# Layer 0 of a two-layer decoder: two differential heads moved ahead of the sparse heads' projections, a sparse pair moved to the end

## The chip, the cores and the metric

One core of one Trainium2 chip runs the whole program. The metric is the time of one execution on the device in microseconds (us). The kernel before takes 1274.81 us, the median of three runs (1271.99 to 1275.66). TensorE (PE in the rows) multiplies matrices and also transposes, PEld is its loading of weights, VectorE is DVE, ScalarE is ACT, GpSimd is POOL, and SyncE (SP) issues all transfers here.

## The reference

Two post-norm decoder layers over 512 tokens of width 1024, in float32. Only layer 0's mixer is touched by the change:

```python
h = x @ w_in_even[li]
qa, ka, va, qn, kc, vc, ksl, vsl, kw, vw, g = _split(h, EVEN_SPLITS)
o_a = diff_attention(...)   # 4 heads: softmax 0 minus lam * softmax 1, times v; RMS norm
o_b = nsa_attention(...)    # 8 query heads in 2 groups: compressed keys, selected keys, window
mix = jnp.concatenate([o_a, o_b], axis=-1) @ w_out_even[li]
x = layer_norm(ALPHA * x + mix, ...)
x = layer_norm(ALPHA * x + sqrelu_mlp(x, ...), ...)
```

The four differential heads and the eight sparse heads don't depend on each other. A differential head needs its own q and k columns of `h` and the v columns of its pair of heads. A sparse head needs its group's q, the compressed keys and values (made from `kc`, `vc` by a small MLP over windows of 32 tokens), two more pairs of k and v, and the gates `g`. With 512 tokens the selection keeps all blocks, so the second and the third branch are plain causal attention. Layer 1 is a forgetting attention of 16 heads and another MLP; its code and its place stay as they are.

## The kernel before

Matmuls run in a float32 format that keeps fewer bits, so each operand is split into a high and a low part (`split`, L112; `unit`, L130) and each product takes three matmuls (L180 to L182). A projection of 256 columns ("chunk") is 96 matmuls of 128x256, in two PSUM banks of 48. Its weights come as two transfers of 512 KB into `wraw` (two buffers, `RB`), ACT makes the high part (L144) and DVE or POOL the low part (L145).

Layer 0's attention is a list of tasks, recorded in the order of `EVEN_ORDER` (L39):

- `W`: projects the inputs of the compression and lays out windows (in two buffers of tag "p"); `C`: the compression MLP, whose weights `w1` come in eight transfers of 512 KB into buffers of tag "v" (four in all, L681); it reads the windows, and its matmuls are full float32 (L687).
- `Q0`, `Q1`: the q of a sparse group (four buffers of tag "q", six in all). `B0`, `B1`: k and v of the second and third branch, the gates with `B1`. Their v take one "v" buffer each for the rest of the attention.
- `c0`, `c1`: the compressed branch's softmax of a group. `P00`, `P01`, `P10`, `P11`: a pair of sparse heads (group, pair): four softmaxes, then `fold` (L306) and `split_y` (L312) into a row block of the output projection's operand.
- `D0` to `D3`: q and k of a differential head. `V01`, `V23`: v of two such heads (two "v" buffers each). `H0` to `H3`: the head itself, two softmaxes, their difference, the product with v, the norm.

A softmax (L262) is, for four blocks of 128 queries, two matmuls into a bank of tag "s", a masked minimum on DVE (L274) and an exp on ACT (L275); it takes one of two "p" buffers. `scale_p` (L316) scales three blocks on POOL (L321) and one on DVE (L323). `transpose_p` (L278) is ten transposes on TensorE (L288), each group of them split into two parts by ACT (L114) and DVE (L116). `stacks_q` and `stacks_k` (L233, L250) split the transposed q and k out of PSUM. `rope` (L564) turns 16 of 64 channels in eight small operations for two blocks of tokens.

PSUM has two banks under each of four tags: "g" for projections and the output projection, "s", "t" and "o". The transposes of a differential head's q and k go to tags that depend on the head (L904): head 0 "g" and "g", head 1 "o" and "g", head 2 "t" and "g", head 3 "t" and "s".

```python
for k in EVEN_ORDER:
    if k == "c0":
        lo_engine[0] = rope_engine[0] = G
    ...
    elif k[0] == "D":
        got[k] = diff_qk(*['gg', 'og', 'tg', 'ts'][int(k[1])])
    ...
    if k in _EVEN:
        ahead()
```

Up to `c0` the low parts of weights (L145) and the rope run on DVE, from there on on POOL. `ahead()` (L607) fetches and splits the weights two chunks ahead. The first two chunks of the list are fetched before the attention (L1031 to L1037).

The list is not the order of execution. A scheduler takes the recorded instructions and sets, for each engine, one fixed order by its own model of time, with buffers given out as they come free; on the chip each engine works through its own list in that order and waits at an instruction whose inputs are not there. So the matmuls of the projections stand between those of the heads. The matmuls of the output projection's first half (L335 to L337) need the first four row blocks in the order in which `EVEN_ORDER` finishes them (`EVEN_KBS`, L45); they are evacuated at L340 with the input x added. The second half (L357 to L359) needs the other four, then follow the layer norm and the MLP.

Of the kernel before, what the change touches and what calls it, by code (L numbers as in the profile page):

```python
# [35 lines left out]

EVEN_ORDER = "W C Q0 B0 B1 c0 D1 V01 P01 P00 D0 Q1 H0 c1 H1 P10 D3 P11 D2 V23 H3 H2".split()  # L39
_EVEN = {"W": [(2048, 256)], "B0": [(2304, 256)], "B1": [(2560, 280)], "Q0": [(1536, 256)], "Q1": [(1792, 256)],  # L40
         "V01": [(1024, 256)], "V23": [(1280, 256)]}
for _h in range(4):
    _EVEN[f"D{_h}"] = [(128 * _h, 128), (512 + 128 * _h, 128)]
EVEN_CHUNKS = [_EVEN[k] for k in EVEN_ORDER if k in _EVEN]
EVEN_KBS = [{"H": 0, "P": 4}[k[0]] + (int(k[1:], 2) if k[0] == "P" else int(k[1])) for k in EVEN_ORDER if k[0] in "HP"]  # L45
FOX_GROUPS = [3, 0, 1, 2]
# [14 lines left out]
def tile_trunk(ctx: ExitStack, tc: tile.TileContext, x, xt_in, ln_gain, ln_bias, w_up, w_down, w_ie, w_oe, lam_p, subln,  # L61
# [539 lines left out]
    def even_attention(ap, mh, ml):  # L601
# [289 lines left out]
        got = {}  # L891
        for k in EVEN_ORDER:
            if k == "c0":
# [241 lines left out]
```

## Time and profile before

| what | us |
|---|---|
| median of three runs | 1274.81 |
| the profiled execution, its whole time | 1273.6 |
| its span, first to last instruction | 1271.5 |
| PE busy | 1237.5 (97%) |
| PEld busy | 1079.2 (85%) |
| DVE busy | 878.2 (69%) |
| ACT busy | 647.3 (51%) |
| POOL busy | 301.2 (24%) |

The chain that ended last is PE for 86% of the span. Matmuls overlap in the pipeline, so a PE that counts as busy may still run thin; the weight loads of the same matmuls, one each, show that better: where PEld is idle, TensorE was waiting between matmuls. Layer 0's attention and the first part of its output projection take the first 308 us of the span. TensorE's granted clock is 0.994 of full speed over the whole span.

### The profile page before, as it was taken

The page shows a single profiled execution, that of the slowest core. Times are in us where ns is not written, and L with a number is a line of the kernel's source. Part 1 is how long each engine was busy: PE and PEld are TensorE (multiplying, and loading weights), DVE is VectorE, ACT ScalarE, POOL GpSimd, SP SyncE. Part 2 cuts the span into 40 slices and gives each one's busy share as a digit, 9 for nine tenths or more (in the row PEclk, how much of TensorE's full clock was granted, in tenths as well). Part 3 has the DMA queues.
Part 4 walks back from the last instruction along what each step waited for, and adds up shares of the span by engine and source line. Part 5 has one row for each costly group of instructions (what it writes and reads, how often), then busy time and mean ns, then how long its engine had stood idle before and what let it go on. Part 6 is the DMA issues. An engine that isn't in the chain of part 4 may idle for free.

```text
span 1271.5 us, 18398 instructions
## 1 busy us (share of the span) xinstructions
PE 1237.5 (97%) x7046; PEld 1079.2 (85%) x7046; DVE 878.2 (69%) x1602; ACT 647.3 (51%) x1185; POOL 301.2 (24%) x321
## 2 busy tenths in 40 slices
PE   7999998998999999999998999999999999999997
PEld 7999897898988888888887889889988888888886
DVE  5476768787859478495456788879767948669454
ACT  5266766764355454454423576767334445354530
POOL 1125565354200000000044354556510000000012
PEclk9999999999999999999999999999999999999999
DMA  7321121034414405234014322323630522505201
GB/s 274 114 87 54 34 67 35 5 129 138 167 61 132 133 25 175 67 96 146 17 50 150 101 84 92 92 88 129 231 112 23 182 84 68 164 34 159 73 17 50
DMA packets 46758, 125.15 MB, mean 98 GB/s; under 512 B 4672, under 2 KB 5184, under 8 KB 46672
## 3 DMA queue, kind: packets, MB, share of 16 engines
q1 hardware_dynamic: 46672, 123.99, 30.3%
q8 instruction: 55, 0.90, 0.3%
q14 instruction: 31, 0.25, 0.1%
HBM read 119.75 MB, written 4.23 MB: 98 GB/s over the span
## 4 chain that ended last, share of the span: by engine, by line
PE 86%; DVE 6%; DMA 3%; ACT 2%; issue 1%; POOL 1%; SPq 0%; DVEq 0%; ACTq 0%; POOLq 0%
PE g L193 11%; PE g L194 11%; PE g L195 11%; PE g L180 4%; PE g L181 4%; PE g L182 4%; PE s L478 3%; PE t L288 3%; PE s L479 3%; PE s L480 2%; DMA wraw<-w_up 2%; PE s L270 2%; PE o L480 2%; PE t L478 2%; PE o L478 2%; PE o L479 2%
## 5 line engine op out<-in xcount | busy, mean ns | idle before, releaser
L194 PE MATMUL g<-big,wlo 128*128 128x512 f32 x608 | 236.8, 391 | 0.0
L195 PE MATMUL g<-big,whi 128*128 128x512 f32 x608 | 236.6, 390 | 0.0
L193 PE MATMUL g<-big,whi 128*128 128x512 f32 x608 | 236.3, 390 | 0.0
L144 ACT ACTIVATE whi<-wraw 128x1024 fp32r<-128x1024 f32 (+3 forms) x120 | 125.3, 1045 | 112.5 <-DMA wraw<-w_up 37.1
L212 POOL TENSOR_TENSOR ve<-ve,nhalf 128x1 f32<-128x1 f32 x16 | 15.9, 991 | 647.0 <-DVE ve L211 647.0
L145 DVE TENSOR_TENSOR wlo<-wraw,whi 128x1024 fp32r<-128x1024 f32 (+2 forms) x69 | 84.3, 1228 | 96.5 <-ACT whi L144 96.4
L145 POOL TENSOR_TENSOR wlo<-wraw,whi 128x1024 fp32r<-128x1024 f32 (+2 forms) x51 | 123.4, 2425 | 94.6 <-ACT whi L144 82.3
L195 PEld LDWEIGHTS g<-big,whi 128*128 128x128 f32 x608 | 114.2, 188 | 23.6
L193 PEld LDWEIGHTS g<-big,whi 128*128 128x128 f32 x608 | 114.2, 188 | 23.2 <-issue 0.2
L194 PEld LDWEIGHTS g<-big,wlo 128*128 128x128 f32 x608 | 114.1, 188 | 23.1
L180 PE MATMUL g<-whi,big 128*128 128x256 f32 (+2 forms) x416 | 120.3, 289 | 0.6 <-DVE fz L946 0.4
L182 PE MATMUL g<-whi,big 128*128 128x256 f32 (+2 forms) x416 | 119.6, 287 | 0.0
L181 PE MATMUL g<-wlo,big 128*128 128x256 f32 (+2 forms) x416 | 119.1, 286 | 0.0
L414 DVE TENSOR_TENSOR wlo<-wdr,whi 128x1024 fp32r<-128x1024 f32 x72 | 87.4, 1218 | 44.4 <-ACT whi L413 44.4
L275 ACT ACTIVATE p<-p,sm 128x128 f32<-128x128 f32 (+3 forms) x160 | 89.2, 558 | 45.7 <-DVE sm L274 44.5
L395 ACT ACTIVATE big<-g 128x512 f32<-128x512 f32 x64 | 38.2, 597 | 134.4 <-PE g L195 134.4
L413 ACT ACTIVATE whi<-wdr 128x1024 fp32r<-128x1024 f32 x72 | 75.9, 1055 | 48.2 <-PE t L480 29.6
L321 POOL TENSOR_TENSOR p<-p,rs 128x128 f32<-128x128 f32 (+2 forms) x108 | 71.5, 688 | 93.2 <-DVE rs L970 40.4
L180 PEld LDWEIGHTS g<-whi,big 128*128 128x128 f32 x416 | 79.1, 190 | 2.2 <-ACT fv L114 0.6
L182 PEld LDWEIGHTS g<-whi,big 128*128 128x128 f32 x416 | 79.1, 190 | 0.7 <-issue 0.4
L181 PEld LDWEIGHTS g<-wlo,big 128*128 128x128 f32 x416 | 79.1, 190 | 0.6
L116 DVE TENSOR_TENSOR ptl<-t,pth 128x384 fp32r<-128x384 f32 (+1 forms) x108 | 63.1, 595 | 21.1 <-ACT pth L114 20.4
(313 smaller groups left out, 3093.0 us busy)
## 6 DMA issues: line engine op xcount, KB each, us to landing
wraw<-w_up SPq DMA_DIRECT2D x64, 512.0 KB, 3.7
wdr<-w_down SPq DMA_DIRECT2D x64, 512.0 KB, 4.7
wraw<-w_io SPq DMA_DIRECT2D x22, 512.0 KB, 3.3
wraw<-w_ie SPq DMA_DIRECT2D x18, 512.0 KB, 3.7
v<-w SPq DMA_DIRECT2D x8, 512.0 KB, 5.2
wraw<-w_oe SPq DMA_DIRECT2D x8, 512.0 KB, 3.6
cb<-c_dram SPq DMA_DIRECT2D x16, 256.0 KB, 3.2
wraw<-w_oo SPq DMA_DIRECT2D x8, 512.0 KB, 3.4
```

Of the source, the lines that this page charges most:

```text
L144: A.activation(hi[:, c], raw[:, c], AF.Copy)
L145: (eng or lo_engine[0]).tensor_tensor(lo[:, c], raw[:, c], hi[:, c].bitcast(F32), op=ALU.subtract)
L180: T.matmul(bv[:, tt], xh, h, start=first, stop=False)
L181: T.matmul(bv[:, tt], xh, l, start=False, stop=False)
L182: T.matmul(bv[:, tt], xl, h, start=False, stop=last)
L193: T.matmul(b[:, a:e], h[:, cs], xh, start=k == 0, stop=False)
L194: T.matmul(b[:, a:e], l[:, cs], xh, start=False, stop=False)
L195: T.matmul(b[:, a:e], h[:, cs], xl, start=False, stop=k == 7)
L275: A.activation(pv, pv, AF.Exp, bias=sm[:, i:i + 1], scale=-1.0, accum_out=sm[:, 4 + i:5 + i])
L413: A.activation(hi, r, AF.Copy)
L414: V.tensor_tensor(lo, r, hi.bitcast(F32), op=ALU.subtract)
L478: T.matmul(bv, hh, us[m][0][:, k], start=first, stop=False, skip_group_check=True)
```

## The change

One line, the list of tasks:

```diff
-EVEN_ORDER = "W C Q0 B0 B1 c0 D1 V01 P01 P00 D0 Q1 H0 c1 H1 P10 D3 P11 D2 V23 H3 H2".split()
+EVEN_ORDER = "D0 V01 D1 H0 W C H1 Q0 B0 B1 c0 P00 D2 P01 V23 H2 Q1 c1 P10 D3 H3 P11".split()
```

The host packs the weights by the same list, so each chunk still is one contiguous block, now in another order. The first two chunks fetched are those of D0 and V01 instead of W and Q0. The point from which rope and low parts run on POOL (`c0`) comes after D0, V01, D1, W, Q0, B0 and B1 instead of after W, Q0, B0 and B1: the ropes of D0 and D1 and the low parts of six more units of weights run on DVE. The first half of the output projection takes H0, H1, P00 and P01 instead of P01, P00, H0 and H1; the last block is P11 instead of H2, and its low part is made by DVE (L822).

No instruction is added on TensorE. What stands where, on the engines:

TensorE at the end of the first projection, before. `g_34` is the second bank of W, `t_36` and `t_40` take its transposes, `g_66` is the first bank of the second chunk, Q0:

```order
L181 MATMUL g_34_206<-big_11_85,big_6_74 128x256
L182 MATMUL g_34_206<-big_11_85,big_7_75 128x256
L623 MATMUL t_36_260<-ident_2_69,nat_33_204 128x128 x2
L623 MATMUL t_40_278<-ident_2_69,nat_33_204 128x128 x2
L180 MATMUL g_66_431<-big_14_120,big_4_72 128x256
L181 MATMUL g_66_431<-big_14_120,big_4_72 128x256
```

The same place now. `g_36` is the second bank of D0, `g_40` and `g_43` take the transposes of its q and k, `g_56` is the first bank of the second chunk, V01; `nat_33` and `nat_37` are the two halves of D0 after the rope:

```order
L181 MATMUL g_36_217<-big_11_85,big_6_74 128x256
L182 MATMUL g_36_217<-big_11_85,big_7_75 128x256
L623 MATMUL g_40_279<-ident_2_69,nat_33_204 128x128 x2
L623 MATMUL g_43_290<-ident_2_69,nat_33_204 128x128 x2
L623 MATMUL g_40_279<-ident_2_69,nat_37_266 128x128
L623 MATMUL g_43_290<-ident_2_69,nat_37_266 128x128
L623 MATMUL g_40_279<-ident_2_69,nat_37_266 128x128
L623 MATMUL g_43_290<-ident_2_69,nat_37_266 128x128
L180 MATMUL g_56_321<-big_14_120,big_4_72 128x256
```

Before, the second chunk's matmuls followed two pairs of transposes into "t"; now they follow all eight, and both banks of tag "g" are taken by the transposes.

DVE at the same place, now: the rope of D0's second half (L575 to L579) ends here, L145 makes the low parts of D1's weights, L246 and L258 empty `g_40` and `g_43`:

```order
L579 TENSOR_TENSOR nat_37_266<-rp1_38_269,rp2_39_270 128x4x16 x2
L145 TENSOR_TENSOR wlo_50_310<-wraw_48_307,whi_49_309 128x1024
L145 TENSOR_TENSOR wlo_53_316<-wraw_51_313,whi_52_315 128x1024
L246 TENSOR_TENSOR q_41_284<-g_40_279,q_41_284 64x512
L246 TENSOR_TENSOR nka_44_295<-g_43_290,nka_44_295 64x512
L258 CAST nkb_45_296<-nka_44_295 64x512
L246 TENSOR_TENSOR q_42_287<-g_40_279,q_42_287 64x512
L246 TENSOR_TENSOR nka_46_301<-g_43_290,nka_46_301 64x512
```

Before, DVE stood here with the low parts of V01's counterpart and a copy for W out of "t" (`y_38`), and no projection's bank waited for it:

```order
L145 TENSOR_TENSOR big_15_121<-wraw_17_126,big_15_121 128x1024
L667 COPY y_38_266<-t_36_260 64x511
L145 TENSOR_TENSOR wlo_46_299<-wraw_44_296,whi_45_298 128x1024
L145 TENSOR_TENSOR wlo_49_305<-wraw_47_302,whi_48_304 128x1024
L667 COPY y_39_272<-t_36_260 64x511
```

Bank `g_40` now comes free at the second L246 of q, behind two L145.

TensorE where the first half of the output projection runs out, before. `g_688` is its last bank, `o_633` takes H3's transposes, `g_715` is the first bank of the second half, `t_648` and `t_651` belong to H2:

```order
L335 MATMUL g_688_3884<-whi_685_3853,big_18_130 128x256
L336 MATMUL g_688_3884<-wlo_686_3854,big_18_130 128x256
L887 MATMUL o_633_3518<-ident_2_69,ft_626_3475 128x128
L337 MATMUL g_688_3884<-whi_685_3853,big_19_131 128x256
L887 MATMUL o_633_3518<-ident_2_69,ft_626_3475 128x128
L357 MATMUL g_715_3955<-whi_694_3917,big_20_132 128x256
```

The same place now, in the middle of P10; `o_515` is P10's second head, `g_716` the second bank of the second half, `s_567` to `s_570` are H3's first softmax:

```order
L337 MATMUL g_688_3884<-whi_685_3853,big_19_131 128x256
L357 MATMUL g_715_3955<-whi_694_3917,big_20_132 128x256
...
L303 MATMUL o_515_2978<-pth_546_3093,v_225_1465 128x128
L304 MATMUL o_515_2978<-ptl_547_3094,v_225_1465 128x128
L357 MATMUL g_715_3955<-whi_694_3917,big_20_132 128x256
L358 MATMUL g_715_3955<-wlo_695_3918,big_20_132 128x256
L357 MATMUL g_716_3982<-whi_700_3929,big_20_132 128x256
L358 MATMUL g_716_3982<-wlo_701_3930,big_20_132 128x256
L270 MATMUL s_567_3264<-nka_563_3256,q_559_3242 128x128
L271 MATMUL s_567_3264<-nkb_564_3257,q_559_3242 128x128
```

Before, the product of H3 was done when the first half ran out, and one head was left. Now all of H3 and all of P11 are left, with 36 matmuls of the second half among them.

## Rows read from the trace of the kernel before

**Rows 1.** Windows: length, busy PE, PEld, DVE, ACT, POOL, granted clock, DMA
```profile
34.00:91.00 57.00, 56.80 (x478) 56.06 (x478) 32.81 (x115) 22.09 (x53) 7.72 (x15) 1.00 0.30 98
91.00:127.40 36.40, 36.24 (x281) 34.32 (x279) 22.26 (x60) 23.18 (x58) 20.80 (x30) 1.00 0.19 59
127.40:142.20 14.80, 12.93 (x82) 9.96 (x80) 13.15 (x37) 12.64 (x33) 10.95 (x20) 1.00 0.22 73
142.20:199.10 56.90, 56.90 (x463) 56.11 (x462) 37.94 (x109) 37.77 (x96) 32.10 (x61) 1.00 0.12 38
199.10:234.60 35.50, 29.93 (x179) 23.96 (x176) 31.81 (x95) 27.16 (x79) 14.98 (x17) 0.95 0.10 31
271.00:292.40 21.40, 21.40 (x175) 21.14 (x175) 19.75 (x51) 13.77 (x39) 8.83 (x7) 1.00 0.26 75
292.40:308.10 15.70, 12.06 (x78) 10.29 (x77) 9.64 (x21) 6.72 (x18) 5.18 (x5) 0.89 0.22 62
```

**Rows 2.** PE in order of time at 127 and 142 us: start, us
```profile
127.41 0.38 PE L623 MATMUL g<-ident,nat 128*128 128x128 f32 x2
...
142.16 0.36 PE L180 MATMUL g<-whi,big 128*128 128x256 f32 x1
```

**Rows 3.** PE in order of time, where the first chunk ends
```profile
21.34 0.60 PE L623 MATMUL t<-ident,nat 128*128 128x128 f32 x4
21.69 0.36 PE L180 MATMUL g<-big,big 128*128 128x256 f32 x1
```

**Rows 4.** ACT in order of time, 15 to 27 us
```profile
16.27 2.00 ACT L144 ACTIVATE big<-wraw 128x1024 fp32r<-128x1024 f32 x2
21.54 0.60 ACT L654 ACTIVATE nat<-g 128x512 f32<-128x512 f32 x1 [3.27 <-PE g L182]
```

**Rows 5.** DVE in order of time, 15 to 25 us
```profile
17.36 1.23 DVE L145 TENSOR_TENSOR big<-wraw,big 128x1024 fp32r<-128x1024 f32 x1 [1.96 <-ACT big L144]
...
18.63 1.22 DVE L145 TENSOR_TENSOR big<-wraw,big 128x1024 fp32r<-128x1024 f32 x1
```

**Rows 6.** DVE by line and form, 20 to 100 us: busy, mean ns
```profile
L579 DVE TENSOR_TENSOR nat<-rp,rp 128x64 f32<-128x64 f32 x4 | 0.9, 217 | 0.0
```

**Rows 7.** DMA issues of the page: KB, us to landing
```profile
wraw<-w_ie SPq DMA_DIRECT2D x18, 512.0 KB, 3.7
v<-w SPq DMA_DIRECT2D x8, 512.0 KB, 5.2
```

**Rows 8.** DVE by line and form, 100 to 345 us
```profile
L310 DVE TENSOR_TENSOR y<-o,ft 64x512 f32<-64x512 f32 x8 | 5.5, 682 | 0.8 <-ACT ft L309 0.8
...
L258 DVE CAST nkb<-nka 64x512 fp32r<-64x512 f32 x8 | 3.4, 422 | 0.3
...
L145 DVE TENSOR_TENSOR wlo<-wraw,whi 128x1024 fp32r<-128x1024 f32 x2 | 2.4, 1217 | 0.0
...
L246 DVE TENSOR_TENSOR q<-g,q 64x512 fp32r<-64x512 f32 x2 | 1.4, 688 | 0.1
```

**Rows 9.** PE in order of time, after a wait near the end of H2
```profile
296.22 0.43 PE L357 MATMUL g<-whi,big 128*128 128x256 f32 x1 [2.11 <-DVE big L340]
296.45 0.41 PE L358 MATMUL g<-wlo,big 128*128 128x256 f32 x1
```

**Rows 10.** DVE by line, 199 to 234 us
```profile
L274 DVE CUSTOM_DVE_ANT_0 p<-s,K 128x128 f32<-128x128 f32 (+3 forms) x23 | 10.6, 474 | 1.7 <-PE t L288 0.9 <-PE s L271 0.6
L116 DVE TENSOR_TENSOR ptl<-t,pth 128x384 fp32r<-128x384 f32 (+1 forms) x15 | 8.6, 595 | 0.0
```

**Rows 11.** POOL in order of time, 283 to 296 us
```profile
283.66 2.39 POOL L145 TENSOR_TENSOR wlo<-wraw,whi 128x1024 fp32r<-128x1024 f32 x1 [5.67 <-issue]
286.22 1.99 POOL L321 TENSOR_TENSOR p<-p,rs 128x128 f32<-128x128 f32 x3 [0.17 <-DVE rs L853]
```

**Rows 12.** DVE line L853: xcount, duration ns min/median/max, first and last start
```profile
L853 DVE TENSOR_SCALAR rs<-rs,lam x4: 218/230/1578, 166.5 to 284.5; 128x4 f32<-128x4 f32 x4
```

**Rows 13.** DVE in order of time, 284 to 286 us
```profile
284.50 1.58 DVE L853 TENSOR_SCALAR rs<-rs,lam 128x4 f32<-128x4 f32 x1
```

## The prediction, made before the changed kernel was run

> **What bounds the kernel now.** I read the page first: PE is busy for 97% of the span and is 86% of the chain that ended last, so a saving on another engine counts only where PE runs thin. Since matmuls overlap in the pipeline, I looked for thin places by PEld, which has one weight load for each matmul: its idle time inside a stage is time that TensorE lost there. The windows of the attention [rows 1] show three kinds of stage. From 142.2 to 199.1 us PEld is idle for 56.9 - 56.11 = 0.79 us and 463 matmuls pass, 0.123 us each: TensorE sets the pace. From 127.4 to 142.2 it is idle for 14.8 - 9.96 = 4.84 us: between the transposes at 127.41 and the next matmul of a projection at 142.16 [rows 2], D0's transposes hold both banks of tag "g", so nothing of a projection can run. From 199.1 to 234.6 it is idle for 35.5 - 23.96 = 11.54 us: this is H1 and P10 without a matmul of a projection between them, and DVE, busy for 31.81 of 35.5 us (90%), sets the pace. The stage at the end, 292.4 to 308.1, loses 15.7 - 10.29 = 5.41 us, in which H2 ends alone. So PE's loss in the attention is a matter of where softmaxes stand without a projection's matmuls beside them, and the change decides just that.
>
> **The change part by part.** TensorE gets the same instructions in another order, and from the second half of the output projection on the order is as before. So I sum the lost time that goes and the lost time that comes.
>
> *What goes.* The three stages above leave the order: D0's transposes no longer stand at 127, H1 and P10 now have matmuls of other tasks among theirs, and H2 isn't last. 4.84 + 11.54 + 5.41 = 21.8 us. TensorE's own work in them stays.
>
> *What comes, a: the front.* Now D0 is first. Before, the second chunk started at 21.69, when TensorE had put W's transposes into "t" [rows 3]. Now both "g" banks are D0's transposes, and V01's first matmul waits until DVE has emptied the first. Its chain: D0's last matmul ends like W's, at 21.34 [rows 3]; ACT's copy ends at 21.54 + 0.60 = 22.1 [rows 4]; the rope of the second half is 8 operations of 0.217 us [rows 6], to 23.9; four more transposes take the 0.35 us of rows 3, to 24.3. But on DVE two L145 for D1's weights stand ahead of the evacuation. They need a `wraw` buffer, free when DVE has finished the L145 of the second chunk at 17.36 + 1.23 = 18.6 and 18.63 + 1.22 = 19.85 [rows 5]; a landing takes 3.7 us [rows 7], so 22.3 and 23.6; ACT's high part takes 1.0 (2.00 for two [rows 4]), so 23.3 and 24.6; DVE, done with the rope at 23.9, ends the L145 at 25.1 and 26.3. Then come L246 for q, L246 for k, the cast L258 and the second L246 of q, 0.69 + 0.69 + 0.42 + 0.69 [rows 8], to 28.8. V01 starts at 28.8 instead of 21.69: 7.1 us, less 0.35 for transposes that TensorE did later before. To the 6.8 comes the clock. After a wait of 2.11 us matmuls of 256 columns came 0.23 us apart (296.22 to 296.45 [rows 9]) and not 0.12, and in that stage the granted clock was 0.89 [rows 1]: 2 x 0.11 x 15.7 = 3.5 us at the lower level (1.2 for 2.4 GHz), half of them lost, 1.7. I take 8.5. The lower bound leaves the two L145 out of the way and the clock up: 26.1 - 21.69 = 4.4. The upper lets these transfers take the 5.2 us of w1's [rows 7], 1.5 more: 10.
>
> *b: shorter stretches without a projection.* Counted in the new order of TensorE, four stretches of 26 to 34 rows have softmaxes or heads alone, 118 rows together. The stretch from 199 to 234.6 has 138 rows and lost 11.54 us, 0.084 each: 118 would lose 9.9. But one of 27 rows in the order of before lies in the stage from 142.2 to 199.1, which lost 0.79 in all [rows 1]. A short one is bridged by work already queued. I take half, 5, with 0 and 9.9 as ends.
>
> *c: the tail.* H3 and P11 now stand after the first half of the output projection, with 36 of its second half's matmuls among them. They are six softmaxes: 24 of L274 and 16 of L116. The stretch from 199 to 234.6 has 23 and 15 [rows 10], so I take its loss, 11.5. Behind it stands the drain of the last block, which nothing covers: POOL's scaling of 1.99 [rows 11], the last transposes and their split, L310 of 0.68 [rows 8], the two halves of the split for the output projection. Part of this chain was at the end of H2 too. I estimate 3.5 us more than what the stretch holds, and take 15. The ends are 11.5 (no drain) and 20 (twice the drain, and the clock once more).
>
> The sum is 8.5 + 5 + 15 - 21.8 = **+6.7 us**. The profiled execution took 1273.6, so 1280.3; it lies 1.2 under the median of 1274.8, against which I forecast 1281.5. The low ends give 4.4 + 0 + 11.5 - 21.8 = -5.9, or 1269; the high ones 10 + 9.9 + 20 - 21.8 = +18, or 1293.
>
> *Moved at no price.* The ropes of D0 and D1 (16 operations of 0.217 each, 3.5 us a head) and six L145 of 1.22 go from POOL to DVE in the front. There DVE is busy for 32.81 of 57 us [rows 1], and this fills it without making it the bound, but for the two L145 in (a). If that cover is gone, 7 to 14 us of DVE would stand in the way. On SP's queue six transfers of w1 stand behind two "v" buffers that V01 used to take later; the transfer behind them is D2's second unit, many chunks ahead of its use.
>
> *A rule that speaks for the change.* POOL's L145 ran from 283.66 to 286.05 (2.39 us [rows 11]), and DVE's L853, an operation on four numbers with a median of 0.230, took 1.58 and ended at 286.08 [rows 12, 13]. So a POOL operation can hold up DVE for its length. The Trainium skill, "SBUF — State Buffer", section "Who interferes with whom", states it as a lock: the two engines share a pair of ports, and the one that starts first keeps it for the whole instruction while the other fully blocks. The row agrees in this instance; the other three L853 escaped. By the rule six L145 less on POOL could spare DVE at most 6 x 1.35 = 8.1 us, and at the average over the four L853 (a third) some 2.5; where DVE paces TensorE, the sum would then be +4.2. I leave it out of the sum, since these six leave the stages in which TensorE sets the pace.
>
> **The rivals.** *A, faster.* Heads start on DVE long before the sparse projections end, so DVE may be far ahead by the tail and TensorE not thinned there. In the stage from 271 to 292.4, also with H3 in it, PEld lost 21.4 - 21.14 = 0.26 us [rows 1]. With that and the drain the tail costs 4 instead of 15, and the sum is -4.3: 1270.5. It decides if DVE is busy under some 80% of the tail (in 271 to 292.4 it was 19.75 of 21.4, 92%, but with projections' matmuls to fill TensorE). Against it: six softmaxes need their minima and splits inside the tail, and those matmuls are gone.
>
> *B, no change.* The wait in front costs 1 instead of 8.5, because TensorE there waits for the first weights in any case and V01's later start is made up in a later wait for weights; the sum is -0.8: 1274. For it: in the first 34 us everything waits for transfers. Against it: V01's weights are there before the banks are, and from 34 us on PEld lost just 0.94 in 57 us [rows 1], so there is nothing later to give back.
>
> *C, much slower.* C now runs with V01 alive in two of the four "v" buffers, so w1's eight transfers use two. One pair's matmuls must end before the next lands, 5.2 us [rows 7] against the little that is in between; at 3.5 us exposed for each of three pairs that is +10.5 on my sum: 1292. It decides if no other work stands between the pairs. For it: H1, whose softmaxes want the "p" buffers that hold C's windows, can't fill in. Against it: B0 and Q0 can be placed there.
>
> **How the numbers follow.** The forecast has a chance of 0.45, with a range of its own of 1276 to 1287; A 0.24, B 0.20, C 0.11. About 0.3%, 3.8 us, can be told from no change. A and nothing else is faster: 0.24. B is the same: 0.20. The forecast and C are slower: 0.56. The range for 8 in 10 goes from 1269 to 1293, by the sums of the low and the high ends, and leaves out the better half of A and the worse half of C.
>
> **What would show it.** Of (a): V01's first L180 at about 29 us, with PE waiting for DVE's L246 and a granted clock under 1 behind it. Of the part that goes: no stretch of 14 us at both "g" banks, none of 35 us without a projection around 200. Of (b): PEld's loss inside the four short stretches, 0 to 10 us in all. Of (c): the last 36 us of the attention with PEld idle for about 15 and DVE busy for 90%, and POOL's scaling in the chain at the end. The attention would then end near 315 instead of 308. The forecast is wrong if PEld loses less than 5 us in that tail (A), if V01 starts before 24 us (B), or if PE waits on w1 for more than 8 us (C).

## The result, and the profile after

The changed kernel takes 1324.72 us (median of 4 runs), the kernel before 1275.24 beside it: ratio 1.0395, 95% interval 1.0369 to 1.042. It is slower by some 49.5 us, where +6.7 was forecast; the time lies 32 us above the range.

The windows of both kernels up to the end of the second half of the output projection (columns as in [rows 1]), of before and then of after:

```profile
0.00:328.00 328.00, 309.14 (x2362) 292.37 (x2363) 229.78 (x612) 192.46 (x467) 137.85 (x199) 0.99 0.30 100
328.00:1271.50 943.50, 928.34 (x4687) 786.85 (x4685) 648.42 (x990) 454.88 (x718) 163.34 (x123) 1.00 0.31 98
```
```profile
0.00:378.00 378.00, 335.61 (x2356) 312.89 (x2357) 233.40 (x651) 195.28 (x468) 112.88 (x160) 0.90 0.26 87
378.00:1323.50 945.50, 929.12 (x4692) 787.92 (x4690) 648.48 (x992) 454.57 (x718) 163.32 (x123) 1.00 0.29 98
```

Of the 50 us in this part, 65.11 - 35.63 = 29.5 are idle time of PEld, and 312.89 - 292.37 = 20.5 are the same weight loads (2357 and 2363 records) taking longer: the granted clock fell from 0.99 to 0.90. Behind this part 2 us differ. So two columns hold the whole difference: how long TensorE waits between matmuls, and how long it then runs at the lower clock.

Where TensorE waits, in six windows of after; the third row is no wait but the stretch behind one:

```profile
20.97:28.99 8.02, 1.59 (x11) 0.90 (x10) 5.94 (x15) 6.10 (x10) 0.00 (x0) 0.85 0.58 196
117.56:140.95 23.39, 13.06 (x60) 10.12 (x58) 17.33 (x78) 9.36 (x28) 1.39 (x2) 0.60 0.07 23
140.95:146.01 5.06, 5.06 (x22) 5.06 (x22) 3.54 (x10) 2.87 (x7) 0.00 (x0) 0.50 0.00 0
237.19:271.00 33.81, 28.19 (x163) 24.89 (x161) 21.94 (x61) 18.10 (x50) 11.61 (x16) 0.77 0.32 110
302.14:310.77 8.63, 3.88 (x26) 2.92 (x24) 7.20 (x10) 5.49 (x10) 1.66 (x1) 0.95 0.23 64
313.83:339.26 25.43, 22.09 (x107) 17.39 (x107) 21.07 (x67) 17.30 (x57) 7.20 (x11) 0.74 0.00 0
344.29:356.31 12.02, 7.69 (x38) 5.92 (x38) 5.99 (x14) 6.09 (x14) 1.96 (x3) 0.86 0.00 1
```

PEld is idle for 7.1 us in front, 13.3 at 117 to 141, 8.9 at 237 to 271 and 5.7 + 8.0 + 6.1 = 19.9 in the tail. That is 49.2 us; less the 21.8 us that the prediction saw go, it makes 27.4 of the 29.5. In the front, TensorE in order of time (what [rows 3] show of before):

```profile
28.99 0.55 PE L180 MATMUL g<-big,big 128*128 128x256 f32 x1 [5.40 <-DVE q L246]
29.34 0.41 PE L181 MATMUL g<-big,big 128*128 128x256 f32 x1
29.56 0.41 PE L182 MATMUL g<-big,big 128*128 128x256 f32 x1
```

V01 starts at 28.99 (28.8 was forecast), and its matmuls start 0.22 us apart. The largest new wait, at 117 to 141, is 29 rows of TensorE's order long, like the short stretches of the prediction's term b, but nothing like this size was forecast for it. TensorE, then ACT, in that stretch:

```profile
118.85 0.65 PE L704 MATMUL o<-pch,ft 128*64 128x64 f32 x8 [1.00 <-DVE ft L700]
123.67 0.37 PE L719 MATMUL t<-ident,ft 64*128 64x64 f32 x1 [4.17 <-DVE ft L716]
...
132.68 0.66 PE L887 MATMUL o<-ident,ft 128*128 128x128 f32 x2 [0.83 <-DVE ft L884]
...
139.77 0.45 PE L623 MATMUL o<-ident,nat 128*128 128x128 f32 x1 [0.80 <-DVE nat L579]
```
```profile
138.15 0.38 ACT L738 ACTIVATE nat<-g 128x256 f32<-128x256 f32 x1 [0.89 <-PE o L623]
```

In order of time these are the end of C (L704, L719), then H1's product and norm (L887), then Q0's transposes (L623), each a short step that waits for DVE, and all in "o" or "t". ACT can copy B0's bank (L738) only when these transposes have freed a "nat" buffer, so both "g" banks stay full and the projection of B1, broken off at 117.56, goes on at 140.95, at a clock of 0.50 until 146. C stands there because it is late: before, its matmuls of L687 started at 34.2 to 48.9 us. POOL laying out the compression's windows, the transfers of w1 on SP, and C's matmuls (duration in ns, first and last start):

```profile
80.93 1.46 POOL L670 TENSOR_TENSOR p<-y,pe 128x256 f32<-128x256 f32 x2 [17.18 <-issue]
```
```profile
89.97 17.14 SPq L683 DMA_DIRECT2D v<-w  x6
```
```profile
L687 PE MATMUL t<-p,v x128: 217/275/275, 88.0 to 113.2; 128*128 128x64 f32 x128
```

The windows take both "p" buffers, which H0 has until its transposes, from 72 us on; six transfers of w1 go out between 90 and 107 as pairs of "v" buffers come free; H1's softmaxes need "p" again when C has read it.

What this does to the order shows in counts. Instructions of the exps (L275, two for each of 96 blocks of queries), before (all done by 300) and after, stretch by stretch:

```profile
0.00:140.00 140.00, 15.01 (x48) 1.00 0.38 128
140.00:200.00 60.00, 15.55 (x48) 1.00 0.11 36
200.00:240.00 40.00, 15.11 (x48) 0.96 0.09 27
240.00:300.00 60.00, 15.35 (x48) 0.97 0.27 89
```
```profile
0.00:140.00 140.00, 10.29 (x32) 0.91 0.35 116
140.00:200.00 60.00, 11.12 (x36) 0.92 0.16 54
200.00:240.00 40.00, 10.95 (x35) 1.00 0.15 53
240.00:300.00 60.00, 13.28 (x42) 0.86 0.21 71
300.00:360.00 60.00, 15.24 (x48) 0.81 0.11 34
```

At 240 us before has 24 blocks left, after 45; and after has no matmul of the projections left there (L180 from 240 to the end of the attention: none; before 21, and as many of L181 and of L182). From then on only the output projection's matmuls stand beside softmaxes.

### The profile page after: what moved, and what is told of

It is laid out like the page before. It is cut to its first block, busy times and chain, and to the rows that moved or that the text cites. A ratio compares the mean times of both kernels' runs of the same rounds, so it can differ in the third digit from the quotient of the medians.

```text
span 1323.5 us, 18399 instructions
## 1 busy us (share of the span) xinstructions
PE 1264.7 (96%) x7046; PEld 1100.8 (83%) x7046; DVE 881.9 (67%) x1641; ACT 649.8 (49%) x1185; POOL 276.2 (21%) x282
## 4 chain that ended last, share of the span: by engine, by line
PE 80%; DVE 6%; ACT 2%; DMA 1%; issue 1%; POOL 0%; DVEq 0%; SPq 0%; ACTq 0%; POOLq 0%
PE g L193 11%; PE g L194 11%; PE g L195 11%; PE t L288 3%; PE s L478 3%; PE g L180 3%; PE s L479 2%; PE g L182 2%; PE g L181 2%; PE s L480 2%; PE o L479 2%; PE o L478 2%; PE t L478 2%; PE o L480 2%; PE s L270 2%; PE s L271 2%
## 5 line engine op out<-in xcount | busy, mean ns | idle before, releaser
L144 ACT ACTIVATE whi<-wraw 128x1024 fp32r<-128x1024 f32 (+3 forms) x120 | 125.5, 1046 | 108.4 <-DMA wraw<-w_up 29.5
L145 DVE TENSOR_TENSOR wlo<-wraw,whi 128x1024 fp32r<-128x1024 f32 (+2 forms) x75 | 90.9, 1215 | 100.8 <-ACT whi L144 100.5
L145 POOL TENSOR_TENSOR wlo<-wraw,whi 128x1024 fp32r<-128x1024 f32 (+2 forms) x45 | 108.4, 2412 | 89.9 <-ACT whi L144 83.2
L180 PE MATMUL g<-whi,big 128*128 128x256 f32 (+2 forms) x416 | 122.7, 295 | 1.4 <-ACT nat L654 1.0
L275 ACT ACTIVATE p<-p,sm 128x128 f32<-128x128 f32 (+3 forms) x160 | 89.2, 558 | 68.0 <-DVE sm L274 67.0
L181 PE MATMUL g<-wlo,big 128*128 128x256 f32 (+2 forms) x416 | 121.1, 291 | 0.0
L182 PE MATMUL g<-whi,big 128*128 128x256 f32 (+2 forms) x416 | 120.6, 290 | 0.0
L180 PEld LDWEIGHTS g<-whi,big 128*128 128x128 f32 x416 | 80.9, 194 | 4.1 <-ACT nat L654 1.3
L181 PEld LDWEIGHTS g<-wlo,big 128*128 128x128 f32 x416 | 80.9, 194 | 0.9 <-issue 0.4
L182 PEld LDWEIGHTS g<-whi,big 128*128 128x128 f32 x416 | 80.7, 194 | 0.7 <-issue 0.4
L116 DVE TENSOR_TENSOR ptl<-t,pth 128x384 fp32r<-128x384 f32 (+1 forms) x108 | 63.2, 596 | 22.6 <-ACT pth L114 21.8
```

Of the source, the lines that this page charges most:

```text
L144: A.activation(hi[:, c], raw[:, c], AF.Copy)
L145: (eng or lo_engine[0]).tensor_tensor(lo[:, c], raw[:, c], hi[:, c].bitcast(F32), op=ALU.subtract)
L180: T.matmul(bv[:, tt], xh, h, start=first, stop=False)
L181: T.matmul(bv[:, tt], xh, l, start=False, stop=False)
L182: T.matmul(bv[:, tt], xl, h, start=False, stop=last)
L275: A.activation(pv, pv, AF.Exp, bias=sm[:, i:i + 1], scale=-1.0, accum_out=sm[:, 4 + i:5 + i])
```

## The experiments

All medians stand beside runs of the kernel before on the same chip; "ratio" is to before. Two versions are compared by their medians, and the medians of before beside them go from 1272.9 to 1275.2. So a difference between two versions is known to some 4 us: the 5.5 of e3 and the 2.8 of g2 below shrink to 3.1 and 1.2 when each is taken against its own runs of before, and are not clear of that; those of e1 and e4 hardly are.

**Front and tail by themselves.** `e2_d0_ts`:

```diff
-['gg', 'og', 'tg', 'ts']
+['ts', 'og', 'tg', 'ts']
```

> The changed kernel, but D0's transposes go to the banks t and s instead of both g. Theory: V01's first matmul no longer waits for DVE's evacuation, it starts at 22 to 23 us instead of 29.0, the clock doesn't fall there, and the time falls by 8 to 11, to 1314 to 1317. Rival (the front is bound by the transfers of the weights, the wait only moves to D1's or W's weights): the start moves but the time falls by less than 4.

Measured: 1314.51, ratio 1.0317 (1.0292 to 1.0342), 10.2 less than the changed kernel. The first matmul of V01 follows D0's transposes at once, at full clock:

```profile
20.21 0.38 PE L623 MATMUL s<-ident,nat 128*128 128x128 f32 x2
20.35 0.36 PE L180 MATMUL g<-big,big 128*128 128x256 f32 x1
```

So the wait for the "g" banks cost some 10, near the 8.5 forecast. `e5_tail_only`, on the kernel before:

```diff
-... H1 P10 D3 P11 D2 V23 H3 H2
+... H1 P10 D2 V23 H2 D3 H3 P11
```

> The kernel before, with its list changed only behind P10: D2 V23 H2 D3 H3 P11 instead of D3 P11 D2 V23 H3 H2, so that H3 and P11 end the attention as in the changed kernel. Theory (the new tail costs on its own what stands in the changed kernel from 302 to 356 us, about 20 us of idle weight loads and 11 us of granted clock, less the 11.5 and 4 of the stretches that before has): 8 to 18 us slower than before, 1283 to 1293. Rival A (the tail costs nothing once the front is as before, since DVE is ahead): within 4 us of before. Rival B (P11 as the last task saves the drain of H2): faster by 3 or more.

Measured: 1289.58, ratio 1.0124 (1.01 to 1.0148), 16.7 slower than before, as the theory said. The two stretches at its end:

```profile
279.50:300.63 21.13, 17.30 (x97) 13.10 (x95) 17.96 (x63) 14.37 (x50) 7.54 (x12) 0.92 0.09 25
305.91:320.32 14.41, 10.20 (x46) 7.20 (x45) 7.45 (x21) 7.13 (x19) 1.96 (x3) 0.75 0.00 0
```

In them PEld is idle for 8.0 + 7.2 us, much like in the last two windows of the changed kernel (8.0 and 6.1). The tail is a cost of its own.

**The stretch at 117 to 141.** `e1_natb`, with two "nat" buffers for the other tasks instead of three (`NB = 2`) and in `branch`:

```diff
-tl = new(ap, "nat", [P, 2, 256], bufs=NB)
+tl = new(ap, "natb", [P, 2, 128], bufs=2)
```

> The changed kernel, but k of the sparse branches B0 and B1 is copied into two buffers of its own (natb) and the other tasks share two of nat instead of three. Theory 1 (in the stretch from 117.6 to 141.0 us no projection can run because the copy of B0's and B1's banks waits for a nat buffer, which Q0's transposes free only after H1's product has left the o banks): the stretch without a projection goes down from 23.4 to under 12 us and the time by 8 to 15, to 1310 to 1317. Rival 1 (TensorE's list itself puts the end of C, H1's product and norm and Q0's transposes in a row, whatever the buffers): a stretch of 20 us or more stays, time 1320 to 1330.

Measured: 1317.13, ratio 1.0347 (1.0318 to 1.0375), 7.6 less. But the stretch stayed:

```profile
121.10:147.15 26.05, 18.03 (x84) 15.44 (x83) 18.55 (x82) 10.68 (x31) 1.39 (x2) 0.56 0.00 0
```

It is 26.05 us long with 26.05 - 15.44 = 10.6 idle: the time just misses theory 1, the stretch speaks for rival 1. The "nat" buffer alone doesn't make the stretch. Where the 7.6 us come from is not shown, since two things were changed at once.

`e3_h1_late` (list: `... H0 W C Q0 B0 B1 c0 H1 P00 ...`):

> The changed kernel with H1 behind c0 in the list instead of ahead of Q0. Theory (H1's product and norm, chained with the end of C and Q0's transposes, make the stretch from 117.6 to 141.0 us, 13.3 us of idle weight loads and a clock at half for 24 us): the stretch goes and the time falls by 15 to 22, to 1303 to 1310. Rival (two softmaxes and a product need their time on DVE wherever they stand, and the stretch only moves): falls by less than 6.

Measured: 1319.25, ratio 1.0372 (1.0334 to 1.0409), 5.5 less, not clear of noise: the rival. The stretch shrank to C's end and the transposes behind it, and another one, 15.5 us long, came at 224; 7.5 + 7.0 us are idle in the two:

```profile
114.47:124.14 9.67, 3.84 (x22) 2.19 (x20) 8.41 (x54) 2.29 (x8) 0.00 (x0) 0.66 0.00 1
224.11:239.65 15.54, 10.66 (x67) 8.54 (x65) 12.04 (x40) 11.31 (x33) 7.03 (x9) 1.00 0.53 198
```

`e8_w1_once`: the eight products of C read one loaded block of w1 (`if j == 0 and c == 0:` ahead of the tile and its DMA), so seven of the eight transfers are left out.

> The changed kernel, but only the first of w1's eight blocks is loaded and used for all eight products of C (the output is wrong by that; the matmuls are the same). Theory 3 (C runs from 88 to 113 us instead of 34 to 49 because it has two v buffers and its transfers come one pair at a time, so that its end and H1 come when the sparse projections are used up): the stretch without a projection at 117 to 141 us goes, and the time falls by 12 to 22, to 1303 to 1313. Rival (the p buffers alone set C's and H1's start, the transfers only spread C among projections that run anyway): falls by less than 6, to 1319 or more.

Measured: 1312.35, ratio 1.0301 (1.0259 to 1.0342), 12.4 less. C's matmuls and what is left of the stretch:

```profile
L687 PE MATMUL t<-p,v x128: 217/275/275, 88.3 to 103.5; 128*128 128x64 f32 x128
```
```profile
120.00:133.58 13.58, 7.62 (x42) 5.62 (x40) 10.46 (x45) 6.84 (x23) 1.39 (x2) 0.74 0.25 78
```

C's last matmul starts at 103.5 instead of 113.2, and 13.3 us of idle become 8.0: the stretch shrank, but it did not go. `g1_c_early` (`D0 D1 W C V01 H0 H1 Q0 ...`) and `g3_c_early_ts` (the same with D0 in "t" and "s") give C its four buffers in another way:

> The changed kernel with W and C ahead of V01 and H0 (D0 D1 W C V01 H0 H1 Q0 B0 B1 ...), so that C has four v buffers and the p buffers for itself, and the two heads still stand ahead of the other sparse projections. Theory 3 (the windows wait 19.6 us for H0's p buffers, C is late, H1 waits for C): the serial stretch goes and the time falls by 12 to 22, to 1303 to 1313. Rival (heads 0 and 1 must stand somewhere without projections beside them, as the run with the sparse projections first showed): within 6 of 1325.

> The same with D0's transposes in t and s. Theory: another 8 to 11 us less than with both in g, as on the changed kernel. Rival (with C early the front's wait is covered): less than 3 us of difference.

Measured: 1313.05, ratio 1.0297 (1.0264 to 1.033), 11.7 less; and 1308.68, ratio 1.0259 (1.0224 to 1.0295), 4.4 less again. C in g1 and the stretch behind it:

```profile
L687 PE MATMUL t<-p,v x128: 217/275/294, 66.4 to 81.4; 128*128 128x64 f32 x128
```
```profile
118.39:130.70 12.31, 7.03 (x43) 5.36 (x40) 8.52 (x29) 7.03 (x23) 1.38 (x2) 0.76 0.12 39
```

In g1 V01's place is taken by D1, whose first matmul starts at 26.70, 2.3 us earlier than V01 did, so less was to be won there with "t" and "s", and some 2 us of g1's 11.7 belong to the front. C's lateness costs 9 to 12 us, by two edits that differ.

**The middle.** `f2_sparse_first` (`W C Q0 B0 B1 c0 D0 V01 H0 D1 H1 P00 D2 ...`):

> The changed kernel with W C Q0 B0 B1 c0 put back ahead of the differential heads (then D0 V01 H0 D1 H1 and the rest as changed), so that only the head of the list is undone. Theory (the front with the wait at D0 costs 10, the serial stretch at H1 and its like in the middle some 20, and both come from the differential heads ahead of the sparse projections): it falls to 1287 to 1297, close to the 1289.6 of the kernel before with the new tail alone. Rival (the middle's loss comes from the mixing of the other heads, D2 V23 H2 among P00 and P01): 1303 to 1312, only the front's 10 us are won.

Measured: 1326.96, ratio 1.041 (1.0393 to 1.0428): nothing won. My theory and its rival both fell. With the sparse projections back in front, PEld is idle for 8.9 and 12.5 us in two other stretches, at D0's transposes into "g" and at the heads behind their own projections; that these are the same loss moved is a reading, not shown by an edit:

```profile
90.70:101.27 10.57, 2.50 (x16) 1.65 (x14) 3.24 (x6) 5.23 (x10) 6.61 (x10) 0.66 0.31 99
143.85:183.23 39.38, 29.92 (x189) 26.86 (x187) 26.96 (x67) 22.08 (x61) 17.87 (x22) 0.87 0.17 54
```

`g2_ahead` (`D0 V01 D1 W C H0 Q0 B0 B1 H1 c0 D2 P00 V23 P01 Q1 H2 c1 D3 P10 H3 P11`):

> The changed kernel with each projection one head further ahead of its use (D0 V01 D1 W C H0 Q0 B0 B1 H1 c0 D2 P00 V23 P01 Q1 H2 c1 D3 P10 H3 P11). Theory 4 (the loss of the middle is the chain from a projection through rope, transposes and split to the first softmax, exposed where a head follows its projection at once): the time falls by 10 or more, below 1315. Rival (the projections are used up earlier still, and the last heads stand alone for longer): 1322 to 1340.

Measured: 1321.91, ratio 1.0359 (1.0321 to 1.0397), 2.8 less, which is no difference: theory 4 fell too, and the rival is missed by 0.1. `e4_old_tail` (changed up to P00, then `P01 Q1 c1 P10 D3 P11 D2 V23 H3 H2`), and `h1_both` (the same tail behind g3's front):

> The changed kernel with its list behind P00 as before: P01 Q1 c1 P10 D3 P11 D2 V23 H3 H2 instead of D2 P01 V23 H2 Q1 c1 P10 D3 H3 P11. Theory (front, middle and tail add up; the new tail alone cost 16.7 us on the kernel before): the time falls by 12 to 20 from the changed kernel's 1324.7, to 1305 to 1313. Rival (the loss of the middle is handed on to whatever tail there is): within 6 us of the changed kernel, 1319 or more.

> The run with C early and D0 in t and s (1308.7), its list behind P00 as before: P01 Q1 c1 P10 D3 P11 D2 V23 H3 H2. Theory 5 (the losses sit in separate places: front, C and H1, tail, each with its own price): the time falls by 12 to 20, to 1289 to 1297, and 14 to 22 over the kernel before are left for the sparse pairs that start late. Rival (one loss handed on: with 16 of 96 softmax blocks done at 140 us instead of 24, the rest must run without projections at some place): falls by less than 7, as on the changed kernel (5.7).

Measured: 1318.99, ratio 1.0347 (1.0324 to 1.0369), 5.7 less than changed; and 1299.32, ratio 1.019 (1.0158 to 1.0222), 9.4 less than g3. Both fall short of the 16.7 that the tail costs alone, e4 into its rival, h1 between the two: the prices of the places don't add up, and part of a loss is handed on. e4 loses 6.6 + 13.3 us in two stretches of its middle:

```profile
203.77:227.84 24.07, 21.52 (x140) 17.45 (x138) 20.47 (x62) 18.96 (x53) 9.36 (x15) 1.00 0.00 1
238.65:273.67 35.02, 28.66 (x135) 21.71 (x135) 27.44 (x76) 21.94 (x58) 13.76 (x17) 0.78 0.10 30
```

`h2_mix`, on the kernel before:

```diff
-... P01 P00 D0 Q1 H0 c1 H1 P10 D3 P11 D2 V23 H3 H2
+... P01 P00 D0 H0 H1 D2 V23 H2 Q1 c1 P10 D3 P11 H3
```

> The kernel before with only the other heads mixed: H0 H1 D2 V23 H2 ahead of Q1 c1 P10, then D3 P11 H3 at the end. Theory 5 (the differential heads' short softmaxes use up the projections D2, V23 and Q1 early, and P10, P11 and H3 stand alone): 15 to 30 slower than before, 1289 to 1304, with a stretch without a projection of 40 us or more at the end. Rival (mixing costs nothing, what costs is the front and P11 as last task): within 6 of before.

Measured: 1298.41, ratio 1.0187 (1.0163 to 1.021), 23.8 slower, by the order of the heads alone (which also makes H3 the last task instead of H2). The same counts of L275 as above; then those of L180 from 200 to 240, before and in h2; then the last two stretches without a projection, with a short piece of the output projection between them:

```profile
0.00:140.00 140.00, 14.98 (x48) 1.00 0.37 128
140.00:200.00 60.00, 14.93 (x48) 0.91 0.11 36
200.00:240.00 40.00, 6.22 (x20) 0.96 0.20 69
240.00:300.00 60.00, 16.93 (x52) 0.91 0.17 61
```
```profile
200.00:240.00 40.00, 3.15 (x11) 2.14 (x12) 0.96 0.09 27
200.00:240.00 40.00, 19.29 (x64) 12.97 (x64) 0.96 0.20 69
```
```profile
276.29:314.61 38.32, 28.63 (x158) 22.86 (x156) 32.44 (x90) 27.66 (x74) 14.83 (x21) 0.91 0.04 15
```

Up to 200 us it has done as many blocks as before, though with fewer matmuls of projections; from 200 to 240 it does 10 blocks beside 64 matmuls of L180 where before does 24 beside 11. By 240 the projections are used up with 38 blocks left, and 15.5 us are idle in one stretch of 38. This is theory 5's place (though not quite its 40 us).

**The kernel before, changed in one place.** `e7_before_d0_ts` (D0 in "t" and "s"), `f1_v23_early` (`H1 V23 P10 D3 P11 D2 H3 H2`), `h3_h2h3` (`H2 H3` at the end), `h4_h1h0` (`H1 c1 H0`):

> The kernel before with D0's transposes in banks t and s instead of both g. Theory (these transposes hold up the projections from 127 to 142 us and 4.8 us are lost there): 2 to 5 us faster than before, 1268 to 1271. Rival (the work that comes earlier only lengthens the stretch from 199 to 235 us): within 2 us of before, or slower.

> The kernel before with V23 moved ahead of P10 (H1 V23 P10 D3 P11 D2 H3 H2). Theory (the stretch from 199 to 235 us loses 11.5 us because no projection is left for it, and V23 needs only buffers that H1 frees): 3 to 8 us faster than before, 1265 to 1270. Rival (V23's buffers come free too late, the stretch stays, and V23 is missing at the end): 0 to 6 us slower.

> The kernel before with H2 ahead of H3 at the end of the list, no other change. Theory (V23 and D3 are there in time for either, one head stands last in both): within 4 of before, 1270 to 1278. Rival (the head that follows its own projection D2 at once shows the chain of rope, transposes and split): 5 to 15 slower.

> The kernel before with H1 ahead of H0 (Q1 H1 c1 H0): D1 is projected long before D0, so its head needs no projection that was just made. Theory (a head that can start earlier fills TensorE's stretch from 127 to 142 us): 2 to 6 faster than before, 1268 to 1272. Rival (the order of H0 and H1 only shifts the stretch from 199 to 235 us): within 3, or slower.

Measured: 1291.72, ratio 1.0133 (1.0117 to 1.015); 1291.9, ratio 1.014 (1.0117 to 1.0163); 1284.36, ratio 1.0076 (1.0052 to 1.0101); 1274.79, ratio 1.0002 (0.9991 to 1.0014). All four theories fell. h3 lies in its rival's range, 9.8 slower, with 8.8 us idle in a stretch at 287 to 305. In h4, its rival too, the two stretches stay with 5.2 and 11.2 us idle. f1 is slower than even its rival allowed: it has 10.7 us idle in a stretch at 178 to 214 and 10.0 at 298 to 325. e7 tells why a gap can't simply be taken out:

```profile
127.40:142.20 14.80, 14.80 (x115) 13.86 (x114) 6.91 (x24) 7.93 (x23) 10.36 (x24) 1.00 0.21 72
...
197.84:246.99 49.15, 40.67 (x221) 30.92 (x219) 40.89 (x132) 35.59 (x106) 18.39 (x27) 0.86 0.06 20
```

The 4.8 us at 127 to 142 [rows 1] are down to 0.9, but the projections done there are missing later (no L180 from 200 to 240, where before has 11): the stretch of 35.5 us at 199 becomes one of 49, its idle time 18.2 instead of 11.5, its clock 0.86 instead of 0.95. The edit has another side that was not tested by itself: D0's transposes now take banks "t" and "s" from the softmaxes, and by 200 us e7 has done 42 blocks instead of 48. No version beat the kernel before.

## Why the prediction was wrong

- **The front, term a: right.** V01 started at 28.99 for 28.8, by the chain that was worked out, with the lower clock behind it; 8.5 forecast, 10.2 measured (e2). Rival B is out. (The low end of this term, 26.1, leaves out one L246 of its own chain, which gives 26.8; nothing hangs on it.)
- **The tail, term c: right in place, a little small.** 15 forecast, 19.9 of idle time in the three windows, 16.7 when made alone (e5). Rival A is out: DVE was busy for 21.07 of 25.43 us in the main stretch (83%), and TensorE was thin all the same.
- **Term b failed: "A short one is bridged by work already queued. I take half, 5."** The stretches at 117 to 141 and 237 to 271, of 29 rows and of 27 and 26, measured 13.3 + 8.9 = 22.2 us of idle time, over twice the upper end of 9.9. In the first one no work that was queued bridged it: the projection that could have done so waited behind it for its banks. The price by row (0.084) was the wrong measure too: 58 weight loads at 117 to 141 lost 13.3, 0.23 each, and 107 at 314 to 339 lost 8.0, 0.075 each. In the first the rows are a chain, each waiting for DVE or ACT; in the second they are mostly softmaxes that overlap.
- **The clock was priced once, at 1.7 us, and cost 20.5.** The prediction had read in [rows 9] and in the 0.89 of [rows 1] that matmuls come half as fast behind a wait, but in its sum it applied this to the front alone. All six windows with a wait show a clock under 1, 0.60 to 0.95, and the third row has no wait at all and runs at 0.50. By these terms b is 17.2 us short, the tail 4.9 and the clock 18.8, which is 40.9 of the 42.8 us between forecast and result. This adds up idle time and clock, not what edits win back.
- **The removed 21.8 us: gone from their places, but not a gain by itself.** e7 and f1 show that where a projection moves into one gap, another opens. The sum treated stretches as independent; e4 and h1 show that they aren't.
- **Rival C had a cause right and the way wrong.** TensorE hardly waited for w1; but w1 in two "v" buffers, and "p" shared by windows and heads, made C end at 113, and that cost 9 to 12 (e8, g1). The forecast gave it a chance of 0.11 and no place in the sum.

That fewer L145 on POOL would spare DVE was worth 8.1 us at most in the forecast and some 2.5 by the average (6 x 1.35 / 4 = 2.0, rightly). The traces do show DVE spared. In this part POOL is busy for 25.0 us less, and the same operations on DVE take less time; L859, the difference of two softmaxes, before and after:

```profile
L859 DVE SCALAR_TENSOR_TENSOR p<-p,rs,p 128x128 f32<-128x128 f32 (+3 forms) x16 | 13.1, 880 | 0.4
```
```profile
L859 DVE SCALAR_TENSOR_TENSOR p<-p,rs,p 128x128 f32<-128x128 f32 (+3 forms) x16 | 8.8, 607 | 0.3
```

The four L853 take 0.9 instead of 2.3. So the 12.7 us of L145 and rope that came to DVE raised its busy time by just 3.6. That POOL is the reason was not tested by an edit, and no gain in the time can be told.

Of the 49.5 us, 16 went with the front and C (g3) and 9.4 more with the tail (h1). The last 24.7 stay open in their split: h2 shows that another order of the heads alone can cost as much (23.8), and how, but on the kernel before, not on this one.

## What to carry to other kernels

Where TensorE's projections fill the time of softmaxes, count both along the time axis: at 240 us before had 24 softmax blocks left and projections to go with them, h2 had 38 and the changed kernel 45, with none. The count at the moment when the projections run out is not enough by itself: behind the last projection matmul e4 and h1 have 18 blocks left, where before has 17, and they are 44.5 and 24.7 us slower, with thin stretches earlier on. Price a new wait with the lower clock behind it, and a run of short dependent steps by its round trips, not by its instructions. Before moving a task forward, look which buffers it shares with what stood there: the windows and the heads had "p" and "v" in common.

## What had not been expected of the hardware

The lower clock outlasts the wait: from 140.95 to 146.01 TensorE had matmuls without a gap at a granted clock of 0.50, its lower level (1.2 of 2.4 GHz), after 23.4 us in which PEld was busy for 10.1. Not every thin stretch brings it: in e3 PEld was idle for 7.0 of 15.5 us at 224, and the clock stayed at 1.00. In all, the same weight loads took 20.5 us more, 41% of the change.
